# A recurrence's tables and matrices made inside the layers and kept in DRAM, and the second block's sums and low parts all on VectorE

## The chip, the cores and the metric

The kernel runs on one core of one Trainium2 chip. The metric is the device time of one execution in microseconds (us); before the change it is 1783.88 us, the median of 3 runs (1783.5 to 1784.17).

## The reference, cut to what matters

The model has two blocks. The first has two layers, each with three branches (a Mamba-2 scan, a sliding-window attention, a forgetting attention), gates and projections. The second has one layer with an S5 recurrence, a top-k sparse attention, a memory attention, and then a mixture of experts of 32 experts. All inputs are float32, there are 256 tokens of width 1024. The change touches how the S5 recurrence gets its constants:

```python
def s5_branch(u, lam_re, lam_im, log_dt, b_re, b_im, c_re, c_im, d_skip, w_glu):
    lam = lax.complex(lam_re, lam_im)
    dt = jnp.exp(log_dt)[:, None]
    lam_bar = jnp.exp(lam * dt)
    b_bar = ((lam_bar - 1.0) / lam)[..., None] * b
    bu = jnp.einsum('bsgh,gph->bsgp', uf, b_bar)
    _, states = lax.associative_scan(_ssm_combine, (a, bu), axis=1)
    y = jnp.real(jnp.einsum('bsgp,ghp->bsgh', states, c))
    ...
# then, in the same layer: sparse attention, memory attention, three gated up-projections, w_out,
# and hier_moe: for each of 32 experts silu(t @ w_gate[e]) * (t @ w_up[e]) @ w_down[e]
```

Nothing of `lam`, `dt`, `b`, `c` or `positions` depends on the first block, so the constants of the recurrence can be made at any time.

## The kernel before, in words

**Projections.** A weight piece of 512 KB is loaded into `wraw` (5 buffers). ScalarE copies it to the rounded high part `whi` (`wsplit`, L213 to L219) and the low part `wlo` (4 buffers) is the difference; TensorE then runs three matmuls per product (`proj_tok`, `proj_fm`). The difference is taken by VectorE (DVE), or by GpSimd (POOL) for one piece in `share[0]`. SyncE's queue (SP) issues all loads in one order; a load into `wraw` waits until the low part of the piece five before it is done.

**Order.** Each block is a string of steps (`ORDER1` for the two layers, `ORDER2` for block 2), read by `run_steps`. `name,args/k` sets a knob: in block 2 every fourth low part goes to POOL (`SH2 = 4`) or as `/k` says, and for `b` (a recurrence step) the bits of k put the sums before the scans (F, bit 2) and after them (E, bit 1) on POOL. A scheduler then orders each engine's queue by these steps' priorities and its own costs; weight loads get a higher priority.

**The recurrence.** Step `sa` (`sin_args`) makes sines and cosines of all angles on DVE and ScalarE, `sp` (`s5_params`, class `S5`) the decay and the input factor, `prep,q` (L881) the two block-diagonal matrices of a quarter: DVE products, PE transposes (L907, L914) and ScalarE copies. `b,q,i` (`block`, L920) is one of 16 recurrence steps: POOL makes a rotation table of 128 x 512 with three instructions (L937 to L939), PE multiplies, DVE rotates (L949 to L952), scans twice (L954, L955) and rotates back (L956 to L960). `end,q` sums a quarter. Every big tile here is a `unit` of 4 KB per partition, of which there are 16.

**The experts.** `fetch` loads their weights, 384 pieces of 512 KB, into a ring of slots: two tiles of a pool `early`, 6 units, 4 `wx`, the buffers of `wraw`, `whi`, `wlo`, `Thi`, `Tlo` and one row. `ahead,2` at the start and `ahead,6` at the end of `ORDER2` fetch the first 8 pieces; the others follow as slots come free, so most of the ring is filled when block 2 has used its last weights.

Of the kernel before, what the change touches and what calls it, by code (L numbers as in the profile page):

```python
# [45 lines left out]
SH1, SH2 = 0, 4  # L46
# [52 lines left out]
dt cq,1 cw cv,1 ax,0/6 cv,0 cq,0/3 ck,0 bk ck,1/6 ca,0,0 ca,1,0 ad,0 ax,1 ax,2 ca,1,1 g,2,1/6 ax,3/3 as_,0,0/0  # L99
z,2,1/0 ca,0,1 g,2,0/3 ad,1 bq,0/0 as_,0,1/3 z,2,0/0 p,2,0/1 bq,1/0 as_,1,0/2 as_,1,1/2 br,0/1 p,2,1/0 z,0,1/6  # L100
br,1/1 ba,1,0 ba,0,0 ba,0,1 g,0,1 g,1,0/3 z,0,0/6 g,1,1 z,1,0/2 ba,1,1 g,0,0/2 p,0,0/0 z,1,1/4 p,0,1 p,1,0/0
p,1,1/1
""", """
cw cv,1 dt cq,1/6 ck,0 cq,0 ck,1 cv,0/2 bq,0/3 g,2,0 ax,1/2 g,2,1/6 ca,0,0 ca,1,0 bq,1 ca,0,1 ax,2/0 ax,0 z,2,0
ax,3 ad,0 ca,1,1 ad,1 as_,0,0/1 as_,0,1/3 z,2,1 as_,1,0 g,1,0/3 bk/3 br,0 br,1/1 as_,1,1 z,0,0 ba,0,0 p,2,1/0
z,0,1/6 ba,0,1 p,2,0/1 ba,1,0 g,0,1/3 ba,1,1 z,1,1/4 z,1,0/2 g,1,1 g,0,0 p,0,1/0 p,0,0 p,1,0/1 p,1,1/1
# [15 lines left out]
def tile_model(ctx: ExitStack, tc: tile.TileContext, I: dict, out: bass.AP):  # L122
# [7 lines left out]
    early = ctx.enter_context(tc.tile_pool(name="early", bufs=1, side="right"))  # L130
# [269 lines left out]
    def layer(l):  # L400
# [308 lines left out]
        def pr(i, c):  # L709
# [6 lines left out]
            def ev_p(t, ps):  # L716
# [3 lines left out]
                else:  # L720
# [6 lines left out]
                     z=z, g=gate, p=pr)  # L727
# [15 lines left out]
    def sin_args():  # L743
# [22 lines left out]
        rows = wtile([128, 128], F32, name="s5rows", bufs=1)  # L766
# [3 lines left out]
        ld = wtile([128, 2], F32, name="s5ld", bufs=1)  # L770
# [19 lines left out]
        tsm = wtile([128, 2, 16], F32, name="tsm", bufs=1)  # L790
# [23 lines left out]
        cs = wtile([128, 1440], F32, name="cs", bufs=1)  # L814
# [23 lines left out]
    def s5_params(cs, lam, dt):  # L838

        r = wtile([128, 16], F32, name="s5r", bufs=1)  # L840
        V.tensor_mul(r, lam[:, 0], dt)
        exp_acc(r, r)
        nt = wtile([128, 4, 16], F32, name="s5cs", bufs=1)
# [4 lines left out]
        f = wtile([128, 2, 16], F32, name="s5f", bufs=1)  # L848
# [14 lines left out]
    class S5:  # L863


        def __init__(self, cs, r, f):
            self.cs, self.r, self.f = cs, r, f
            self.bT, self.h = {}, {}
            self.pm = wtile([128, 2, 2], F32, name="s5pm", bufs=1)
            nc.sync.dma_start(self.pm.rearrange("p a b -> p (a b)"), I["c_cmask"])  # L870
            self.dsk = wtile([128, 4], F32, name="s5d", bufs=1)
            nc.sync.dma_start(self.dsk, I["d_skip_2"][0].rearrange("(q p) -> p q", p=128))
# [5 lines left out]
        def start(self, u_fm):  # L878
            self.u = u_fm

        def prep(self, q):  # L881

            bs = wtile([128, 2, 4, 16], F32, name="s5b")
            cr = wtile([128, 2, 64], F32, name="s5c")
# [5 lines left out]
            tb = wtile([128, 4, 64], F32, name="s5t", bufs=1)  # L890
# [11 lines left out]
            bT = self.bT[q] = unit().rearrange("p (k n) -> p k n", k=8)  # L902
            bb8 = self.bb.rearrange("p i c n -> p (i c) n")
            for k0 in (0, 4):
# [3 lines left out]
                S.copy(bT[:, k0:k0 + 4, :], tp)  # L908
            z = wtile([128, 2, 2, 64], F32, name="s5z", bufs=1)
# [8 lines left out]
            self.h[q] = [unit() for _ in range(2)]  # L918

        def block(self, q, i):  # L920
            j = 4 * q + i
            E, F = (G if knob[0] & m else V for m in (1, 2))
            full = [128, 2, 16, 16]
            cs = self.cs
# [14 lines left out]
            G.tensor_tensor(tw, tw, tx, op=OP.add)  # L939
            two = [128, 2, 256]  # L940
# [73 lines left out]
    def rope2(dst, src, cs, t, nh):  # L1014
        c, s = (cs[:, k + 512 + 32 * t:k + 544 + 32 * t][:, None, :].to_broadcast([128, nh, 32]) for k in (256, 848))
# [54 lines left out]
    def block2(pair=None):  # L1070
        W = I["w_in_2"][0]
        mpair = xT = xf = kmT = vm = u_fm = s5 = wm = wf = par = None
# [51 lines left out]
        def ev_kv(t, ps):  # L1124
# [3 lines left out]
            rope2(kk[:, 0:1], kn[:, None, :], par[0], t, 1)  # L1128
# [4 lines left out]
            rope2(qr[t][:, 512:768].rearrange("p (h d) -> p h d", h=4), qn.rearrange("p (h d) -> p h d", h=4), par[0], t, 4)  # L1133
# [3 lines left out]
            rope2(kk[:, 0:1], kin[:, None, :], par[0], t, 1)  # L1137
# [167 lines left out]
        def ahead(n):  # L1305
            for _ in range(n):
# [4 lines left out]
                     mn=memory_norm, wm=norm_weights, sa=sines, sp=states, lo=finish_layer, nt=normed, kv=memory_kv,  # L1311
# [8 lines left out]
        for c in range(2):  # L1320
# [13 lines left out]
                 e=lambda: early.tile([128, 1024], F32, name="we", bufs=RAWE),  # L1334
# [427 lines left out]
```

## Time and profile before

| | |
|---|---|
| median of 3 runs | 1783.88 us |
| the profiled execution | 1783.39 us, span 1781.5 us, so 1.9 us lie around the span |
| layers (two of them) | 46 to 960 us of the span |
| block 2 up to the router | 960 to 1310 us |
| experts | 1310 to 1781 us |
| busy: PE, DVE, ACT, POOL | 94%, 56%, 39%, 17% of the span |
| the chain that ended last, by engine | PE 69%, DMA 17%, DVE 9%, POOL 2% |

The busy shares are means over stages with different limits: PE is busy all the time in the layers, DVE has its highest share in block 2, and the DMA queues are full from 1310 us on. So each stage is read by itself below. In the rows, "PE proj L149" is a matmul that accumulates into a tile `proj` and is issued by line 149; `u` is any unit.

### The profile page before, as it was taken

What the parts mean: (1) busy time and instruction counts of PE and PEld (TensorE: products, weight loads), DVE (VectorE), ACT (ScalarE), POOL (GpSimd) and SP (SyncE); (2) the same over time, 40 slices, a digit from 0 to 9 for tenths busy, and PEclk for the clock granted to TensorE, in tenths of its full rate; (3) what the DMA queues carried; (4) which work ended last, traced back from release to release, by engine and by line L of the source; (5) the groups of instructions that cost most, each with busy time, mean ns of one, the idle gap of its engine ahead of it and who ended that gap; (6) DMA issues with size and microseconds to landing.
All of it is one profiled execution on the core that took longest, in us unless ns stands there. A gap on an engine that the chain in (4) does not pass through costs nothing.

```text
span 1781.5 us, 23994 instructions
## 1 busy us (share of the span) xinstructions
PE 1680.2 (94%) x8941; PEld 1245.8 (70%) x8941; DVE 997.4 (56%) x1642; ACT 695.9 (39%) x1331; POOL 297.4 (17%) x242
## 2 busy tenths in 40 slices
PE   7999999999999999999998997887879999999998
PEld 6999888888798999888876876764634443434342
DVE  6656656666673568675668797899631221212121
ACT  5455555644444656556536553311311110101010
POOL 0111116220102101321013423374100000000000
PEclk9999999999999999999999998998989999999999
DMA  8644445455566544453565543123799999999997
GB/s 268 197 143 138 135 148 147 144 166 165 166 175 180 168 118 132 137 165 108 186 198 152 146 141 95 48 71 106 248 409 376 410 409 409 409 409 409 409 409 300
DMA packets 185592, 389.65 MB, mean 219 GB/s; under 512 B 28736, under 2 KB 65792, under 8 KB 185472
## 3 DMA queue, kind: packets, MB, share of 16 engines
q1 hardware_dynamic: 185472, 388.08, 64.0%
q8 instruction: 72, 1.18, 0.3%
q14 instruction: 48, 0.39, 0.1%
HBM read 386.98 MB, written 1.05 MB: 218 GB/s over the span
## 4 chain that ended last, share of the span: by engine, by line
PE 69%; DMA 17%; DVE 9%; POOL 2%; issue 2%; ACT 1%; SPq 0%; DVEq 0%; ACTq 0%; POOLq 0%
PE proj L149 45%; PE proj L1574 6%; PE sc L149 5%; PE pv L149 4%; PE sc L1596 3%; DMA Tlo<-in_w_up_dram 2%; DMA whi<-in_w_up_dram 2%; DMA wx<-in_w_up_dram 2%; DMA wraw<-in_w_down_dram 2%; PE tp L386 1%; PE tp L305 1%; DMA u<-in_w_up_dram 1%; DMA u<-in_w_down_dram 1%; DMA wlo<-in_w_up_dram 1%; DVE wlo L217 1%
## 5 line engine op out<-in xcount | busy, mean ns | idle before, releaser
L217 DVE TENSOR_TENSOR wlo<-wraw,whi 128x1024 fp32r<-128x1024 f32 (+1 forms) x278 | 361.0, 1302 | 173.9 <-PE proj L149 120.6
L216 ACT CAST whi<-wraw 128x1024 fp32r<-128x1024 f32 x322 | 337.4, 1051 | 284.1 <-PE proj L149 228.6
L149 PE MATMUL proj<-whi,Thi 128*128 128x512 f32 (+1 forms) x1008 | 396.1, 396 | 11.2 <-ACT u L1277 8.7
L149 PE MATMUL proj<-wlo,Thi 128*128 128x512 f32 (+1 forms) x1008 | 398.5, 396 | 4.0 <-DVE wlo L217 2.5
L149 PE MATMUL proj<-whi,Tlo 128*128 128x512 f32 (+1 forms) x1008 | 394.7, 394 | 0.0
L149 PEld LDWEIGHTS proj<-whi,Thi 128*128 128x128 f32 x1008 | 190.7, 189 | 50.0 <-ACT u L1277 8.9
L149 PEld LDWEIGHTS proj<-wlo,Thi 128*128 128x128 f32 x1008 | 190.6, 189 | 43.5 <-DVE wlo L217 5.7
L149 PEld LDWEIGHTS proj<-whi,Tlo 128*128 128x128 f32 x1008 | 190.5, 189 | 37.7
L217 POOL TENSOR_TENSOR wlo<-wraw,whi 128x1024 fp32r<-128x1024 f32 (+1 forms) x44 | 111.5, 2534 | 404.7 <-PE proj L149 299.8
L149 PE MATMUL proj<-Thi,whi 128*128 128x256 f32 x560 | 158.2, 287 | 2.3 <-DVE u L489 1.6
L149 PE MATMUL proj<-Thi,wlo 128*128 128x256 f32 x560 | 159.0, 285 | 0.0
L149 PE MATMUL proj<-Tlo,whi 128*128 128x256 f32 x560 | 158.2, 285 | 0.0
L1578 DVE SCALAR_TENSOR_TENSOR th<-th,cg,proj 128x512 f32<-128x512 f32 x16 | 12.0, 747 | 212.8 <-PE proj L1574 210.7
L149 PEld LDWEIGHTS proj<-Thi,whi 128*128 128x128 f32 x560 | 107.3, 193 | 3.5 <-DVE u L489 1.8
L149 PEld LDWEIGHTS proj<-Thi,wlo 128*128 128x128 f32 x560 | 108.1, 193 | 0.2
L149 PEld LDWEIGHTS proj<-Tlo,whi 128*128 128x128 f32 x560 | 107.3, 193 | 0.1
L149 PE MATMUL sc<-u 128*128 128x256 f32 (+1 forms) x416 | 98.7, 353 | 6.8 <-DVE u L950 6.4
L1577 ACT ACTIVATE th<-proj,cg 128x512 f32<-128x512 f32 x16 | 11.0, 687 | 191.2 <-PE proj L1574 191.2
L1600 DVE TENSOR_TENSOR u<-sc,u 128x512 fp32r<-128x512 f32 x32 | 22.0, 691 | 109.5 <-ACT u L1599 90.4
L149 PEld LDWEIGHTS sc<-u 128*128 128x128 f32 x416 | 69.1, 194 | 15.2 <-issue 8.7
L377 ACT ACTIVATE P<-sc,nm 128x256 f32<-128x256 f32 (+1 forms) x152 | 63.7, 432 | 38.7 <-DVE nm L370 24.3
L1599 ACT CAST u<-sc 128x512 fp32r<-128x512 f32 x32 | 18.6, 585 | 136.1 <-PE sc L1596 113.5
(467 smaller groups left out, 2537.9 us busy)
## 6 DMA issues: line engine op xcount, KB each, us to landing
wraw<-in_w_in_dram SPq DMA_DIRECT2D x236, 512.0 KB, 3.8
wraw<-in_w_proj_dram SPq DMA_DIRECT2D x48, 512.0 KB, 4.2
u<-in_w_up_dram SPq DMA_DIRECT2D x25, 512.0 KB, 10.2
wraw<-in_w_out_dram SPq DMA_DIRECT2D x24, 512.0 KB, 4.7
u<-in_w_gate_dram SPq DMA_DIRECT2D x24, 512.0 KB, 10.2
wraw<-in_w_up_dram SPq DMA_DIRECT2D x21, 512.0 KB, 10.2
whi<-in_w_down_dram SPq DMA_DIRECT2D x21, 512.0 KB, 10.2
u<-in_w_down_dram SPq DMA_DIRECT2D x21, 512.0 KB, 10.2
```

Of the source, the lines that this page charges most:

```text
L149: T.matmul(o, l, r, start=start, stop=stop)
L216: S.copy(hi[:, :, :n], raw[:, :, :n])
L217: (G if share[0] and scount[0] % share[0] == 0 else V).tensor_sub(lo[:, :, :n], raw[:, :, :n], hi[:, :, :n].bitcast(F32))
L305: T.transpose(ps[:, b, :], src[:, b * 128:(b + 1) * 128], ident)
L377: S.activation(P[:, i * nS:(i + 1) * nS], scv[:, i, :], AF.Exp, bias=nm[:, i:i + 1], accum_out=l_out[:, i:i + 1])
L386: T.transpose(tp[:, j, :], P[:, j * 128:(j + 1) * 128], ident)
L1574: pin(T.matmul(ps[r], xk, w[:, 512 * j:512 * j + 512], start=k == 0, stop=k == 7))
L1577: S.activation(hid, pg, AF.Silu, scale=cg[:, 1:2])
L1578: V.scalar_tensor_tensor(hid, hid, cg[:, 0:1], pu, op0=OP.mult, op1=OP.mult)
L1596: pin(T.matmul(po[c][r], hT[:, k, r], w[:, 512 * c:512 * c + 512], start=k == 0, stop=k == 3))
L1599: S.copy(yh[:, c], po[c])
L1600: V.tensor_sub(yl[:, c], po[c], yh[:, c].bitcast(F32))
```

## The change

- `sin_args` and `s5_params` run in layer 0 (`sa`, `sp`), with tiles of a pool `s5` on the right side of the memory instead of `early`.
- A class `Made` has the steps `cl` (two memsets), `mat,q` (the old `prep`, which then writes the two matrices of 512 KB each to DRAM) and `turn,j` (the three POOL instructions of a rotation table, then a write of 256 KB to DRAM). `mat,0` to `mat,3` and `turn,0` to `turn,7` stand in layer 0, `turn,8` to `turn,15` in layer 1.
- In block 2 `prep,q` loads the two matrices and `block` loads its table (`s5rot`, 3 buffers); the constants of the position rotation are loaded too.
- `SH2` is 0 and `ORDER2` has no `/k`: every low part and every sum of block 2 is on DVE. The three gated sums of L1298 stay on POOL.
- `early` is opened after the layers, where `s5` lay.

```diff
-SH1, SH2 = 0, 4
+SH1, SH2 = 0, 0
 ORDER1 = ["""
-dt cq,1 cw cv,1 ax,0/6 cv,0 cq,0/3 ck,0 bk ck,1/6 ca,0,0 ca,1,0 ad,0 ax,1 ax,2 ca,1,1 g,2,1/6 ax,3/3 as_,0,0/0
+dt cq,1 cw sa cv,1 sp cl ax,0/6 mat,0 cv,0 mat,1 cq,0/3 mat,2 ck,0 mat,3 bk ck,1/6 ca,0,0 ca,1,0 ad,0 turn,0 ax,1
...
 ORDER2 = """
-ahead,2 mn sa sp lo wm nt kv prep,0 u/6 b,0,1/1 keys/6 vk mem_q sel,0 queries/3 mem,0 b,0,0/3 gate,2,1/6 mem,1 b,0,3/1
+ahead,2 mn sp lo wm nt kv prep,0 u b,0,1 keys vk mem_q sel,0 queries mem,0 b,0,0 gate,2,1 mem,1 b,0,3
...
-    early = ctx.enter_context(tc.tile_pool(name="early", bufs=1, side="right"))
+    dram = ctx.enter_context(tc.tile_pool(name="dram", bufs=1, space=bass.MemoryType.DRAM))
+    made = ExitStack()
+    sp = made.enter_context(tc.tile_pool(name="s5", bufs=1, side="right"))
+    early = []
...
+    class Made:
+        def __init__(self):
+            self.rot = [dram.tile([128, 1024], F32, name=f"rot{n}") for n in range(8)]
+            self.mats = [dram.tile([128, 2, 1024], F32, name=f"mats{n}") for n in range(4)]
+            self.misc = dram.tile([128, 144], F32, name="misc")
...
+        def mat(self, q):
...
+            nc.sync.dma_start(self.mats[q][:, 0], bT)
...
+            nc.sync.dma_start(self.mats[q][:, 1], czf)
+        def turn(self, j):
...
+            tw = sp.tile([128, 512], F32, name="s5tw", bufs=1)
+            tx = wtile([128, 512], F32, name="th")
...
             G.tensor_tensor(v4(tw), pairs(256, 592), ca, op=OP.mult)
             G.tensor_tensor(v4(tx), pairs(0, 256), sa, op=OP.mult)
             G.tensor_tensor(tw, tw, tx, op=OP.add)
+            nc.sync.dma_start(self.rot[j // 2][:, 512 * (j % 2):512 * (j % 2) + 512], tw)
...
+        def prep(self, q):
+            b, c = unit(), wtile([128, 1024], F32, name="s5cz", bufs=1)
+            nc.sync.dma_start(b, made_.mats[q][:, 0])
+            nc.sync.dma_start(c, made_.mats[q][:, 1])
...
+        def block(self, q, i):
+            j = 4 * q + i
+            E, F = (G if knob[0] & m else V for m in (1, 2))
+            tw = wtile([128, 512], F32, name="s5rot", bufs=3)
+            nc.sync.dma_start(tw, made_.rot[j // 2][:, 512 * (j % 2):512 * (j % 2) + 512])
...
+    made_ = Made()
     with scoped("b1"):
         layer_out(0, layer(0))
         pair = layer(1)
     lay.close()
+    made.close()
+    early.append(ctx.enter_context(tc.tile_pool(name="early", bufs=1, side="right")))
```

POOL's queue in the middle of block 2, before: tables (L937 to L939), low parts (L217) and the sums before and after the scans (L951, L952, L959, L960) by turns.

```order
L315 TENSOR_TENSOR rstd_10042<-rstd,neghalf 128x8
L937 TENSOR_TENSOR u<-cs 128x512
L938 TENSOR_TENSOR u<-cs 128x512
L939 TENSOR_TENSOR u<-u 128x512
L951 TENSOR_TENSOR u<-u 128x256
L952 TENSOR_TENSOR u<-u 128x256
L217 TENSOR_TENSOR wlo<-wraw,whi 128x1024
L959 TENSOR_TENSOR u<-u 128x256
L960 TENSOR_TENSOR u<-u 128x256
```

The same place after: the last norms, then only the gated sums and the memsets of the expert stage.

```order
L319 TENSOR_TENSOR rstd_10103<-rstd,neghalf 128x4
L319 TENSOR_TENSOR rstd_10239<-rstd,neghalf 128x8
L319 TENSOR_TENSOR rstd_10257<-rstd,neghalf 128x8
L1336 TENSOR_TENSOR u<-u 128x512 x4
L1465 MEMSET wts 128x1 x8
```

All tables, low parts and sums have left POOL's queue there (the numbers behind `rstd` name the tile).

POOL's queue in layer 0 after: `s5tw` is the table's single buffer, so the first product of a table (L949) waits until the table before it has been written to DRAM.

```order
L221 TENSOR_TENSOR wlo<-wraw,whi 128x1024
L951 TENSOR_TENSOR s5tw<-s5tw,th 128x512
L949 TENSOR_TENSOR s5tw<-cs 128x512
L951 TENSOR_TENSOR s5tw<-s5tw,th 128x512
L949 TENSOR_TENSOR s5tw<-cs 128x512
L498 MEMSET u 64x1024 x2
L221 TENSOR_TENSOR wlo<-wraw,whi 128x1024
```

Behind the waiting product stand the memsets of the keys (L498) and a low part; before the change nothing of the tables stood in this part of the queue.

SP's queue in layer 0 after, with the writes of matrices (`mats`) and of the first two tables (`rot`):

```order
L923 DMA mats_102<-u 128x1024
L932 DMA mats_102<-u 128x1024
L902 DMA u<-in_c_im_dram 128x64
L205 DMA wraw<-in_w_in_dram 128x2x512
L952 DMA rot_94<-s5tw 128x512
L205 DMA wraw<-in_w_in_dram 128x2x512 x2
L901 DMA u<-in_b_re_dram 128x4x16
L902 DMA u<-in_c_re_dram 128x64
L901 DMA u<-in_b_im_dram 128x4x16
L902 DMA u<-in_c_im_dram 128x64
L923 DMA mats_103<-u 128x1024
L932 DMA mats_103<-u 128x1024
```

Weight loads (`wraw`) now stand behind writes that wait for ScalarE's copies and POOL's tables.

## Rows read from the trace of the kernel before

**Rows 1.** Busy time by stage: width, each engine, PE clock, DMA share and rate.

```profile
core 0: us, PE busy (x) PEld busy (x) DVE busy (x) ACT busy (x) POOL busy (x), PEclk, DMA share, GB/s
46.00:484.00 438.00, 432.88 (x2542) 382.32 (x2542) 279.67 (x389) 237.32 (x456) 82.48 (x61) 1.00 0.52 155
520.00:960.00 440.00, 438.17 (x2548) 385.29 (x2548) 284.75 (x443) 239.62 (x464) 75.58 (x52) 1.00 0.53 157
960.00:1310.00 350.00, 291.51 (x1333) 225.59 (x1332) 283.54 (x546) 132.14 (x271) 130.36 (x116) 0.93 0.44 138
1180.00:1200.00 20.00, 20.00 (x76) 13.42 (x75) 17.27 (x22) 1.45 (x3) 16.34 (x15) 1.00 0.18 51
1310.00:1490.00 180.00, 173.76 (x864) 75.26 (x865) 35.75 (x74) 18.83 (x34) 0.00 (x0) 0.98 1.02 401
1490.00:1781.00 291.00, 274.45 (x1216) 113.54 (x1212) 56.83 (x104) 27.40 (x48) 0.00 (x0) 0.99 0.99 393
```

**Rows 2.** Chain of waits, block 2, shares of the stretch by line.

```profile
by line: PE proj L149 29.4%; PE pv L149 5.3%; PE sc L149 4.7%; issue 4.4%; DVE wlo L217 4.4%; DVE u L957 3.4%; DVE u L955 3.2%; DVE u L956 2.4%; DVE u L951 2.1%; DVE u L952 2.1%; DVE u L949 2.0%; DVE u L950 1.9%; DVE u L954 1.9%; DMA wraw<-
```

**Rows 3.** Chain of waits, pieces: start us, length us, what.

```profile
967.92 0.68 DVE u L809
...
968.76 1.20 DVE x L1068
...
973.87 0.70 ACT cs L815
...
989.61 0.87 PE tp L1055 x8
...
1083.07 1.00 DVE u L901
1084.08 1.32 DVE u L901
```

**Rows 4.** Single instructions of DVE: start us, length us, line, operation.

```profile
963.45 3.41 DVE L1068 SCALAR_TENSOR_TENSOR x<-x,rstd,rowb 128x1024 f32<-128x1024 f32 x1 [0.24 <-POOL rstd L315]
...
1205.09 0.68 DVE L949 TENSOR_TENSOR u<-sc,u 128x512 f32<-128x512 f32 x1
...
1206.75 0.42 DVE L952 TENSOR_TENSOR u<-u 128x256 f32<-128x256 f32 x1
...
1210.39 0.68 DVE L949 TENSOR_TENSOR u<-sc,u 128x512 f32<-128x512 f32 x1
...
1212.89 1.48 DVE L952 TENSOR_TENSOR u<-u 128x256 f32<-128x256 f32 x1
...
1217.60 0.68 DVE L949 TENSOR_TENSOR u<-sc,u 128x512 f32<-128x512 f32 x1
```

**Rows 5.** Single instructions of POOL, the same stretch.

```profile
1211.63 1.06 POOL L938 TENSOR_TENSOR u<-cs 128x512 f32<-128x512 f32 x1
```

**Rows 6.** DVE groups of block 2: shape, count, busy us, mean ns, idle before.

```profile
L217 DVE TENSOR_TENSOR wlo<-wraw,whi 128x1024 fp32r<-128x1024 f32 x38 | 52.8, 1399 | 6.5 <-PE proj L149 4.9 <-ACT whi L216 1.0 <-issue 0.5
```

**Rows 7.** POOL groups of block 2.

```profile
L217 POOL TENSOR_TENSOR wlo<-wraw,whi 128x1024 fp32r<-128x1024 f32 x10 | 26.1, 2609 | 40.0 <-ACT whi L216 34.3 <-PE proj L149 5.8
L939 POOL TENSOR_TENSOR u<-u 128x512 f32<-128x512 f32 x16 | 21.3, 1334 | 1.1
L938 POOL TENSOR_TENSOR u<-cs 128x512 f32<-128x512 f32 x16 | 20.4, 1276 | 0.0
L937 POOL TENSOR_TENSOR u<-cs 128x512 f32<-128x512 f32 x16 | 19.7, 1234 | 53.4 <-DVE u L957 14.4 <-DVE u L1295 13.8 <-DVE u L960 13.5
```

**Rows 8.** Who waited for whom, block 2: us in total, times, longest.

```profile
DVE u L949 <- POOL u L939: 8.0, 3, 3.0
...
PE tp L914 <- ACT u L908: 4.8, 1, 4.8
```

**Rows 9.** SP's queue over the whole span: waits.

```profile
SPq L201 <- DVE wlo L217: 591.2, 185, 16.8
```

**Rows 10.** DMA issues: KB each, median us to landing.

```profile
out_dram<-x SPq DMA_DIRECT2D x4, 256.0 KB, 3.1
```

More of the change, by code (lines that the diff above doesn't have):

```diff
@@ L726, in layer @@
         steps = dict(dt=a_steps, cw=a_conv, ck=c_k, cq=c_q, cv=c_v, ca=c_att, ax=a_x, ad=a_dt, as_=a_ssd, bq=b_q, bk=b_kv, br=b_rope, ba=b_att,
-                     z=z, g=gate, p=pr)
+                     z=z, g=gate, p=pr, sa=made_.sines, sp=made_.states, cl=made_.clear, mat=made_.mat, turn=made_.turn)
         run_steps(ORDER1[l], steps, SH1)
@@ L876, in __init__ @@
             G.memset(self.cz, 0.0)
[L878 to L884, printed above, removed]
+        def mat(self, q):
+            u = unit()
+            bs = u[:, 0:128].rearrange("p (c i h) -> p c i h", c=2, i=4)
+            cr = u[:, 128:256].rearrange("p (c d) -> p c d", c=2)
+            tb = u[:, 256:512].rearrange("p (c n) -> p c n", c=4)
+            z = u[:, 512:768].rearrange("p (c a d) -> p c a d", c=2, a=2)
             for c, (b_, c_) in enumerate((("b_re_2", "c_re_2"), ("b_im_2", "c_im_2"))):
@@ L917, in prep @@
             S.copy(dst, tp[:, 0:2, :].rearrange("p c (i n) -> p c i n", i=4))
[L918 to L922, printed above, removed]
+            nc.sync.dma_start(self.mats[q][:, 1], czf)
+        def turn(self, j):
+            cs = self.cs
             full = [128, 2, 16, 16]
-            cs = self.cs
             def pairs(k0, stride):
@@ L939, in block, with __init__, start @@
             G.tensor_tensor(tw, tw, tx, op=OP.add)
+            nc.sync.dma_start(self.rot[j // 2][:, 512 * (j % 2):512 * (j % 2) + 512], tw)
+    class S5:
+        def __init__(self):
+            self.bT, self.cz, self.h = {}, {}, {}
+            self.rr = wtile([128, 144], F32, name="s5m", bufs=1)
+            nc.sync.dma_start(self.rr, made_.misc)
+            self.rope, self.r = self.rr[:, 0:128], self.rr[:, 128:144]
+            self.dsk = wtile([128, 4], F32, name="s5d", bufs=1)
+            nc.sync.dma_start(self.dsk, I["d_skip_2"][0].rearrange("(q p) -> p q", p=128))
+        def start(self, u_fm):
+            self.u = u_fm
+        def prep(self, q):
+            b, c = unit(), wtile([128, 1024], F32, name="s5cz", bufs=1)
+            nc.sync.dma_start(b, made_.mats[q][:, 0])
+            nc.sync.dma_start(c, made_.mats[q][:, 1])
+            self.bT[q] = b.rearrange("p (k n) -> p k n", k=8)
+            self.cz[q] = c.rearrange("p (c i n) -> p c i n", c=2, i=4)
+            self.h[q] = [unit() for _ in range(2)]
+        def block(self, q, i):
[3 more added lines that the diff above has]
+            nc.sync.dma_start(tw, made_.rot[j // 2][:, 512 * (j % 2):512 * (j % 2) + 512])
             two = [128, 2, 256]
@@ L1082, in norm_weights @@
             wm = unit_row(I["g_mix_2"][0])
-        def sines():
-            nonlocal par
-            par = sin_args()
         def states():
             nonlocal s5
-            s5 = S5(par[0], *s5_params(*par))
+            s5 = S5()
         def finish_layer():
@@ L1310, in block2 @@
                      vk=positions, ahead=ahead,
-                     mn=memory_norm, wm=norm_weights, sa=sines, sp=states, lo=finish_layer, nt=normed, kv=memory_kv,
+                     mn=memory_norm, wm=norm_weights, sp=states, lo=finish_layer, nt=normed, kv=memory_kv,
                      u=inputs, **{n: lambda *a, n=n: getattr(s5, n)(*a) for n in ("prep", "block", "end")})
```

98 lines of the change are left out of this document (49 added, 49 removed).

## The prediction, made before the changed kernel ran

> **What bounds the kernel now.** I read the busy time by stage first [rows 1]. In the two layers PE is busy 432.9 of 438 us and 438.2 of 440: they are PE-bound, and DVE (64%) and POOL (17 to 19%) work beside it. In block 2 (960 to 1310 us) PE is busy 291.5 of 350 us, DVE 283.5 and POOL 130.4, and PE's granted clock is 0.93 on the mean (stretches at 1.2 GHz between those at 2.4): no engine is full, they wait for each other. From 1310 us on the DMA queues are full (share 1.02 and 0.99, 401 and 393 GB/s), and the chain that ended last runs through weight loads; PE isn't full (274.5 of 291 us). The 384 expert pieces come in one stream that starts when block 2's last weights free their buffers, so the end moves with block 2's end, one for one: a us won in block 2 or lost in the layers is a us of the total.
>
> Then the chain of waits in block 2 [rows 2]: nearly half of it is DVE. The recurrence's lines (L949 to L957) have 1.9 to 3.4% of 350 us each, the low parts 4.4%. Last the single instructions [rows 4, 5]. A recurrence step whose table is not made meanwhile takes 5.30 us on DVE (first rotation at 1205.09, that of the next step at 1210.39) and has all its ten instructions there. The next step, with POOL's table instructions beside it (one at 1211.63), takes 7.21 us (1210.39 to 1217.60): L952 is 1.48 us long instead of 0.42. So POOL's work makes DVE's longer, and this is the reader's main point.
>
> **The change part by part: block 2.**
>
> - Tables gone from POOL: three instructions of 1.234, 1.276 and 1.334 us, 16 times, 61.4 us in all [rows 7]. What they cost is their hold on DVE: 7.21 − 5.30 = 1.91 us a step. L949 has 2.0% of 350 us on the chain, 7.0 us, at 0.64 us visible of each: 11 of the 16 steps lie on it. 11 × 1.91 = 21.0 us. The sums that move from POOL to DVE are in this already, since the 5.30 us step has them all. But in 1180 to 1200 us PE is busy 20.0 of 20 us [rows 1]: what DVE saves there is hidden behind PE, about 3 steps, −5.7 us.
> - DVE's waits for a table, 8.0 us in 3 [rows 8]: gone, if the loads (below) are early.
> - The start of the block: the final norm's L1068 is 3.41 us beside a POOL low part and 1.20 us the next time [rows 3, 4], 2.2 us; two pieces of the sine tables on the chain, 0.68 and 0.70 us. Together 3.6 us.
> - `prep` leaves: PE's wait before L914, 4.8 us [rows 8], and two DVE products on the chain, 1.00 and 1.32 us [rows 3]: 7.1 us.
> - Against it: 11 low parts come from POOL to DVE (10 whole, one smaller). 11 × 1.399 = 15.4 us of DVE [rows 6]. Of DVE's 52.8 us of low parts 15.4 us (4.4% of 350) are on the chain, 29%, so 4.5 us.
>
> Waits removed: 21.0 − 5.7 + 8.0 + 3.6 + 7.1 − 4.5 = 29.5 us. PE's clock comes on top: 7% of 350 us are 24.5 us of lost work, beside 58.5 us in which PE is idle, 0.42 us for each idle one. Part of the low-clock time is idle anyway, so I take half of 29.5 × 0.42: 6 us. Block 2: 35.5 us shorter. Bounds: 8 us (half of the steps that PE doesn't cover, 15.3 us, and nothing else) to 58.5 us (all of PE's idle time).
>
> New in block 2 are loads of 16 tables of 256 KB and 8 matrices of 512 KB, 8 MB; at 401 GB/s some 21 us of the queues, whose share is 0.44 there [rows 1]: room enough. They stand in SP's one queue between weight loads, and a table waits for a buffer whose recurrence step is done. Behind such a wait stand `wraw` loads, and PE waits for those. SP waits for low parts in this way already, 591.2 us in 185 waits, 3.2 us each, and PE hardly notices, since five pieces are loaded ahead [rows 9]. I put 0 on it, 26 us (8 of the 24 loads at 3.2 us) as the bad end.
>
> **The layers.**
>
> - 41 transposes (10 per quarter and one for the parameters) come to PE where it is full. Eight take 0.87 us [rows 3]: 41 × 0.109 = 4.5 us, nearly sure.
> - POOL gets 61.4 us of tables. In the layers PE is idle 5.1 + 1.8 = 7.0 us beside 158.1 us of POOL [rows 1], 0.044 us for each; 61.4 × 0.044 = 2.7 us. The bad end: each of the 16 tables delays one POOL low part by its length, 2.609 us [rows 7], and PE with it: 42 us. Below nothing it can't be, since nothing leaves the layers. I take 2.7, as the row of the same stage.
> - The matrices are now made between DVE, PE, ScalarE and SP early in layer 0. Before, one of the four made PE wait 4.8 us [rows 8]; I take the same once. The ends are 0 and 4 × 4.8 = 19 us. DVE has room for the sines and products: 158 of 438 us are free in the layer [rows 1].
> - A table's first product waits until the last table is written, since there is one buffer. A write of 256 KB takes 3.1 us to land [rows 10]; behind the waiting product stand memsets of the keys and low parts, and PE waits for those when the write is late. Within the 42 us above.
>
> The layers: 4.5 + 2.7 + 4.8 = 12.0 us longer.
>
> **Sum.** 35.5 − 12.0 = 23.5 us. The profiled execution is 1783.39 us (span 1781.5 and 1.9 around it): 1759.9 us. The median shown is 0.5 us above the profiled one, so 1760 us.
>
> **The rivals.**
>
> A, PE becomes the bound and the layers hide all but the transposes. For it: POOL's 130 us leave nearly all, and DVE then has under 270 us to do in block 2 (283.5, less 16 × 1.91 = 31, plus 15.4; `prep` and the sines go too) against PE's 291.5. Against: single chains stay (last recurrence step, `end`, `glu`, the router). Price: the 29.5 us and half of the other 29 us of idle time, 44 us; 1783.4 − 44 + 4.5 = 1744 us.
>
> B, slower: the hold on DVE only moves. POOL's tables meet the low parts of the layers, and there PE has no time to spare. If each of the 16 tables costs PE one POOL low part, 42 us, the layers grow by 4.5 + 4.8 + 42 = 51 us: 1783.4 − 35.5 + 51 = 1799 us. It decides from (35.5 − 9.3) / 16 = 1.6 us a table on. For it: L952's 1.48 us. Against: DVE is idle a third of the layers and POOL four fifths, and PE waits there only 0.044 us per us of POOL. The Trainium skill states such a rule ("SBUF — State Buffer", section "Who interferes with whom"): a DVE instruction with two SBUF inputs and a GpSimd instruction that reads SBUF exclude each other, and the one that comes second is blocked for the whole of the other. The low part has two SBUF inputs, so by that rule the layers pay each table that falls on a due low part; the trace agrees as to L952, while L949, which reads PSUM, stays at 0.68 us beside POOL.
>
> C, the gain is lost inside block 2: table loads make SP late. 35.5 − 26 us there, and the layers' 12.0: 1786 us. For it: one queue. Against: the 3.2 us above, and PE's loads five pieces ahead.
>
> **How the numbers follow.** A change under 0.2% (3.6 us) can't be told from none in this kernel. My forecast, with the sizes as above (1748 to 1776 us), has 0.61; A 0.16; B 0.12; C 0.11, of which half ends within 0.2% and the rest on both sides, slower a little more. Faster 0.79, same 0.07, slower 0.14. The forecast is 1760 us. The range goes to 1740 below, A's time less 4, which leaves 0.07 out, and to 1784 above, which leaves out B and half of C's, some 0.14.
>
> **What would show it.** Right: in block 2 PE busy over 90% at a clock near 0.97, recurrence steps of 5.3 us each, POOL under 30 us, no wait of DVE for a table; layers 8 to 16 us longer, by transposes and one or two waits of PE early in layer 0; the stream of experts shifted as a whole, at the same 390 to 400 GB/s. B shows as PE waiting for low parts (L217's successor) beside table instructions in the layers. C shows as waits of SP for a recurrence step with PE waiting for `wraw` behind it. I am wrong if block 2 shrinks by less than 20 us, or if the layers grow by more than 20.

## The result, and the profile after

The changed kernel takes 1765.46 us (median of 4 runs, 1762.19 to 1768.05) against 1783.69 us for the one before (4 runs, 1782.51 to 1784.17): a ratio of 0.9898, 95% interval 0.9877 to 0.9918. The profiled execution is the 1762.19 us one, its span 1760.4 us. 1760 us was forecast.

Busy time by stage in the changed kernel (width, each engine, PE clock, DMA share and rate); it answers to [rows 1]:

```profile
46.00:484.00 438.00, 424.32 (x2503) 375.72 (x2502) 297.31 (x470) 236.35 (x463) 125.71 (x96) 0.98 0.55 167
520.00:960.00 440.00, 437.32 (x2628) 387.98 (x2627) 286.54 (x411) 238.15 (x463) 83.75 (x56) 1.00 0.55 165
...
1310.00:1490.00 180.00, 176.34 (x876) 75.46 (x877) 37.55 (x75) 20.92 (x36) 0.00 (x0) 1.00 1.02 404
1490.00:1760.00 270.00, 252.32 (x1118) 103.99 (x1114) 51.95 (x97) 25.00 (x44) 0.00 (x0) 0.99 0.98 391
```

The first layer has lost PE time (432.88 busy before, 424.32 now), the second has not, and the expert stream runs at the rate it had. To see where the time went I numbered the matmuls of the helper's line (L149 before, L153 after; 6222 in both traces) by their starts, set each against the one of the same number, and took the difference. Inside block 2 the order is not quite the same (5600 and 6000 fall on other tiles), so those two columns compare how far the work has come; the others fall on the same tiles:

```
matmul no.             200   400   600  1600  2600  4000  4800  5000  5200  5600  6000  6221
before, us            48.8  77.9 107.0 275.1 501.8 721.0 889.1 941.2 998.3 1102  1227  1307
after, later by       +2.7 +20.0 +22.3 +22.3 +24.3 +24.3 +25.9 +23.9 +14.4  -0.2 -18.4 -20.7
```

So there are two large sums of opposite sign. Layer 0 loses 22.3 us over the work that the kernel before has done at 107 us, and the difference then stays. From the block's head (matmul 5000) to the router (6221), 366.0 us become 321.5: block 2 wins 44.6 us. (Two us more are won between 4800 and 5000, where two of block 2's low parts stood on POOL; the layers' loss is 25.9 us ahead of them and 23.9 behind.) The same stretch of both kernels, before and then after:

```profile
941.00:1307.00 366.00, 309.06 (x1416) 239.90 (x1414) 297.30 (x576) 142.14 (x284) 134.55 (x119) 0.94 0.44 138
```

```profile
965.00:1286.50 321.50, 296.94 (x1375) 232.51 (x1373) 250.44 (x510) 132.04 (x266) 20.43 (x35) 0.97 0.55 178
```

PE's idle time falls from 56.9 to 24.6 us, POOL from 134.6 to 20.4, and the clock rises from 0.94 to 0.97. The recurrence in the changed kernel, DVE's single instructions, answers to [rows 4]:

```profile
1194.36 0.69 DVE L991 TENSOR_TENSOR u<-sc,s5rot 128x512 f32<-128x512 f32 x1
...
1196.02 0.42 DVE L994 TENSOR_TENSOR u<-u 128x256 f32<-128x256 f32 x1
...
1199.65 0.68 DVE L991 TENSOR_TENSOR u<-sc,s5rot 128x512 f32<-128x512 f32 x1
```

A step is 5.29 us, and L994 (L952 before, where it took 1.48 us) is 0.42. The waits in block 2 and on SP's queue over the span answer to [rows 8, 9]:

```profile
PE pv L153 <- DMA s5cz<-mats: 3.0, 1, 3.0
```

```profile
SPq L205 <- DVE wlo L221: 564.5, 197, 14.5
...
SPq L981 <- DVE u L999: 38.4, 10, 6.6
SPq L952 <- POOL s5tw L951: 30.2, 13, 4.0
```

No wait for a table's making is left; the loads cost PE one wait of 3.0 us. DVE's low parts in 960 to 1310 us are 60 of mean 1209 ns now. [rows 6] has 38 of 1399 in that window, but the block has moved in it and this view counts two forms; in the stretch from matmul 5000 to 6221 there were 45 on DVE and are 57, the 12 of POOL's, and a whole one takes 1217 ns in place of 1382:

```profile
L221 DVE TENSOR_TENSOR wlo<-wraw,whi 128x1024 fp32r<-128x1024 f32 (+1 forms) x60 | 71.9, 1209 | 12.4 <-PE proj L153 10.6 <-issue 1.3 <-ACT Thi L310 0.4
```

Layer 0 is the other side. Who made PE wait from 40 to 90 us:

```profile
PE tp L921 <- DVE u L915: 6.4, 1, 6.4
PE proj L153 <- DVE u L788: 2.8, 1, 2.8
PE proj L153 <- DVE s5dt L833: 2.2, 1, 2.2
PE proj L153 <- DVE wlo L221: 1.0, 1, 1.0
```

The kernel before waits 1.6 us there. The first wait is for a matrix (L915 puts its entries in place, and the transposes at L921 follow in PE's order), the next two for DVE's work on the projections behind the sines' and parameters' small operations: they end at 50.5 and 57.8 us, each some 0.15 us after the last of three reads of `proj` on DVE (L536), among which the small operations stand. With the waits goes the clock. The two stretches before, then after:

```profile
30.00:60.00 30.00, 28.40 (x180) 25.70 (x179) 25.00 (x42) 14.39 (x20) 2.38 (x1) 1.00 0.82 250
60.00:90.00 30.00, 30.00 (x223) 28.71 (x222) 15.53 (x17) 14.21 (x19) 7.12 (x4) 1.00 0.64 191
```

```profile
30.00:60.00 30.00, 23.98 (x134) 21.05 (x133) 24.20 (x74) 11.04 (x15) 4.30 (x3) 0.92 0.70 201
60.00:90.00 30.00, 23.54 (x132) 20.94 (x132) 25.60 (x59) 12.85 (x18) 9.35 (x6) 0.85 0.38 110
```

0.92 and 0.85 against 1.00 are 2.4 + 4.5 = 6.9 us of work. 12.4 − 1.6 of waiting and 6.9 of clock leave 4.6 of the 22.3 us, about what 40 transposes take at 0.109 us each (4.4). Before the longest wait, POOL and DVE:

```profile
76.76 1.41 POOL L949 TENSOR_TENSOR s5tw<-cs 128x512 f32<-128x512 f32 x1 [2.35 <-ACT cs L822]
78.14 2.06 POOL L950 TENSOR_TENSOR th<-cs 128x512 f32<-128x512 f32 x2
80.16 2.33 POOL L221 TENSOR_TENSOR wlo<-wraw,whi 128x1024 fp32r<-128x1024 f32 x1
82.46 1.25 POOL L951 TENSOR_TENSOR s5tw<-s5tw,th 128x512 f32<-128x512 f32 x1
```

```profile
79.26 0.97 DVE L857 TENSOR_TENSOR s5cs<-s5cs,s5lam 128x16 f32<-128x16 f32 x1
80.27 2.27 DVE L859 TENSOR_TENSOR s5cs<-s5cs 128x16 f32<-128x16 f32 x1
82.57 1.18 DVE L860 TENSOR_TENSOR s5f<-s5cs,s5dt 128x16 f32<-128x16 f32 x1
83.67 0.16 DVE L862 TENSOR_TENSOR s5cs<-s5cs,s5lam 128x16 f32<-128x16 f32 x1
```

An operation on 128x16 numbers (L859, 0.165 us in the kernel before) takes 2.27 us beside POOL's low part of 2.33: it waits for nearly the whole of the other.

### The profile page after: what moved, and what is told of

The parts are those of the page before. It is cut to its first block, busy times and chain, and to the rows that moved or that the text cites. A ratio compares the mean times of both kernels' runs of the same rounds, so it can differ in the third digit from the quotient of the medians.

```text
span 1760.4 us, 24091 instructions
## 1 busy us (share of the span) xinstructions
PE 1677.4 (95%) x8941; PEld 1246.4 (71%) x8941; DVE 987.2 (56%) x1678; ACT 695.0 (39%) x1331; POOL 242.6 (14%) x206
## 4 chain that ended last, share of the span: by engine, by line
PE 73%; DMA 15%; DVE 8%; POOL 1%; issue 1%; ACT 1%; SPq 0%; DVEq 0%; POOLq 0%; ACTq 0%
PE proj L153 48%; PE proj L1612 6%; PE sc L153 5%; PE pv L153 4%; PE sc L1634 3%; DMA whi<-in_w_up_dram 2%; DMA wx<-in_w_up_dram 2%; DMA Tlo<-in_w_up_dram 2%; PE tp L390 1%; PE tp L309 1%; DVE wlo L221 1%; PE tp L1571 1%; DMA u<-in_w_down_dram 1%; DMA wraw<-in_w_down_dram 1%; DMA wlo<-in_w_up_dram 1%
## 5 line engine op out<-in xcount | busy, mean ns | idle before, releaser
L221 DVE TENSOR_TENSOR wlo<-wraw,whi 128x1024 fp32r<-128x1024 f32 (+1 forms) x292 | 374.1, 1286 | 172.0 <-PE proj L153 118.7
L153 PE MATMUL proj<-wlo,Thi 128*128 128x512 f32 (+1 forms) x1008 | 397.8, 395 | 0.0
L153 PE MATMUL proj<-whi,Thi 128*128 128x512 f32 (+1 forms) x1008 | 395.1, 395 | 1.0 <-ACT Thi L310 0.7
L153 PE MATMUL proj<-whi,Tlo 128*128 128x512 f32 (+1 forms) x1008 | 393.3, 393 | 0.0
L153 PEld LDWEIGHTS proj<-whi,Thi 128*128 128x128 f32 x1008 | 190.1, 189 | 39.4 <-ACT Thi L310 1.9
L153 PEld LDWEIGHTS proj<-whi,Tlo 128*128 128x128 f32 x1008 | 189.8, 188 | 37.6 <-DVE Tlo L311 0.2
L153 PEld LDWEIGHTS proj<-wlo,Thi 128*128 128x128 f32 x1008 | 190.1, 189 | 36.8
L153 PE MATMUL proj<-Thi,whi 128*128 128x256 f32 x560 | 160.7, 290 | 5.7 <-DVE u L788 2.8
L153 PE MATMUL proj<-Thi,wlo 128*128 128x256 f32 x560 | 161.2, 289 | 1.0 <-DVE wlo L221 1.0
L153 PE MATMUL proj<-Tlo,whi 128*128 128x256 f32 x560 | 160.8, 289 | 0.0
L221 POOL TENSOR_TENSOR wlo<-wraw,whi 128x1024 fp32r<-128x1024 f32 x30 | 77.4, 2580 | 315.0 <-PE proj L153 205.0
L153 PEld LDWEIGHTS proj<-Thi,whi 128*128 128x128 f32 x560 | 109.5, 197 | 7.0 <-issue 5.4
L153 PEld LDWEIGHTS proj<-Thi,wlo 128*128 128x128 f32 x560 | 110.0, 197 | 1.5 <-DVE wlo L221 1.3
L153 PEld LDWEIGHTS proj<-Tlo,whi 128*128 128x128 f32 x560 | 109.4, 196 | 0.1
L153 PE MATMUL sc<-u 128*128 128x256 f32 (+1 forms) x416 | 97.1, 349 | 3.8 <-DVE u L992 3.8
L153 PEld LDWEIGHTS sc<-u 128*128 128x128 f32 x416 | 68.4, 192 | 11.2 <-issue 4.6
L381 ACT ACTIVATE P<-sc,nm 128x256 f32<-128x256 f32 (+1 forms) x152 | 63.8, 433 | 31.6 <-DVE nm L374 17.4
```

The costliest lines, as they stand in the source:

```text
L153: T.matmul(o, l, r, start=start, stop=stop)
L221: (G if share[0] and scount[0] % share[0] == 0 else V).tensor_sub(lo[:, :, :n], raw[:, :, :n], hi[:, :, :n].bitcast(F32))
L381: S.activation(P[:, i * nS:(i + 1) * nS], scv[:, i, :], AF.Exp, bias=nm[:, i:i + 1], accum_out=l_out[:, i:i + 1])
```

## The experiments

Each was timed in 4 to 12 runs against 9 to 17 of the kernel before on the same chip. "Later by" is the matmul count above, from the profiled runs.

**One part alone, and the other.** The kernel before with this edit of the change (and no `/k` in ORDER2):

```diff
-SH1, SH2 = 0, 4
+SH1, SH2 = 0, 0
```

> The kernel before with one part of the change alone: block 2's sums (22.7 us on POOL before) and low parts of weights (68.4 us) all on DVE, the tables (73.1 us on POOL) still made in block 2, nothing in the layers. Theory 1: POOL's time beside DVE costs whoever makes it, so block 2 gives back in proportion to the POOL time that goes, 91 of 164 us: of the 40 us that block 2 lost in the changed kernel some 22, a time of 1762 us. Rival: the tables' chain is what block 2 waited for and the low parts on DVE fill the place that POOL left; then 5 us or less, 1779 us or more.

1776.77 us, ratio 0.9956 (0.9943 to 0.997): 7 us won, where theory 1 wanted 22 and its rival up to 5. (By the trace POOL had 20 us of sums, 28 of low parts and 61 of tables in block 2, less than the expectation took; by these theory 1 would want 18, and fails as well.) 3.6 us of the gain lie between 5000 and 6221, and 2.0 just ahead, where two low parts stood. The changed kernel with the opposite edit, so that the tables and matrices move alone:

> The changed kernel with the other part alone: tables and matrices made in the layers, but block 2's sums and low parts shared with POOL as before. Layers keep their cost of about 20 us. Theory 1: block 2 gives back in proportion to the 73 of 164 us of POOL time that go, some 18 us, plus the matrices' preparation, 7 us: 1783.7 + 20 - 25 = 1779 us. Rival (the tables' chain is what block 2 waited for): block 2 gives back 35 us or more, 1768 us or less.

1769.84 us, 0.9925 (0.9911 to 0.9939). The tables and matrices win 42.4 us from 5000 to 6221, nearly all of the 44.6; the layers cost 28.0. DVE's operations beside POOL's low parts and sums are 17.3 us longer in that stretch than alone, yet little of it reaches the end. A split in proportion to POOL's time is wrong: moving the tables and matrices out is the gain, and the sums and low parts add 2.2 us to it (4.4 by the medians). So the price of such a hold depends on where it falls; what makes these places cheap was not tested.

**Is it hold or chain?** The changed kernel with idle work on POOL in each step:

```diff
+            du = wtile([128, 512], F32, name="dum", bufs=1)
+            for _ in range(3):
+                G.tensor_tensor(du, tw, tw, op=OP.mult)
             two = [128, 2, 256]
```

> The changed kernel, and in each of block 2's sixteen steps three products 128x512 more on GpSimd, which read the loaded table and write a tile that nobody reads: 48 instructions of 1.1 to 1.4 us, some 60 us of GpSimd beside DVE, and no wait of anybody for them. Theory 1 (what tables in block 2 cost is mostly GpSimd's hold on DVE's operations): block 2 loses a good part of the 33 us that separate it from the kernel with the sums alone moved: 12 to 25 us, 1777 to 1790 us. Rival (it is the chain that waits for a table's products and for the matrices): 4 us or less, up to 1769 us.

1786.19 us, 1.0019 (1.0008 to 1.0029). Up to matmul 5000 it runs as the changed kernel does (+23.3), at 6221 it is 1.2 us later than the kernel before. So it wins 22.1 us in that stretch in place of 44.6: 22.5 us are lost, half of block 2's gain, to work that nobody waits for (20.7 by the medians). PE is idle 38.4 us of the stretch in place of 24.6, and its clock is 0.94 in place of 0.97. What it does to a step, DVE's instructions beside three of the products at 1205.41 to 1209.85:

```profile
1205.41 4.44 POOL L984 TENSOR_TENSOR dum<-s5rot 128x512 f32<-128x512 f32 x3 [3.81 <-DMA s5rot<-rot]
```

```profile
1206.16 1.35 DVE L1001 TENSOR_TENSOR u<-u,s5rot 128x512 f32<-128x512 f32 x1
1207.43 1.52 DVE L1002 TENSOR_TENSOR u<-u,s5rot 128x512 f32<-128x512 f32 x1
1209.06 1.07 DVE L1004 TENSOR_TENSOR u<-u 128x256 f32<-128x256 f32 x1
1210.06 0.41 DVE L1005 TENSOR_TENSOR u<-u 128x256 f32<-128x256 f32 x1
```

They are 0.68, 0.68 and 0.42 us alone. Over the stretch, DVE's operations beside POOL (each against the median of its line alone) are 22.8 us longer; in the kernel before 44.8, in the changed one 1.3. The same place with memsets in place of the products (`G.tensor_copy(du[:, 0:1], tw[:, 0:1])` and eight of `G.memset(du, 0.0)` a step):

> The changed kernel, and in each of block 2's sixteen steps a copy of one column and eight memsets 128x512 on GpSimd into a tile that nobody reads: by the memset 64x1024 of 0.95 us some 60 us of GpSimd again, as in the run with the idle products, but without reading a tile in the state buffer (but for the one column). Theory R (GpSimd holds DVE's operations only where it reads two tiles, as the products do): 3 us or less, up to 1768 us, and DVE's scans and sums keep 0.41 and 0.67 us beside a memset. Rival (any work on GpSimd slows DVE): again some 15 to 22 us, 1780 to 1787 us.

1768.39 us, 0.9917 (0.9903 to 0.993). POOL has 128 memsets of 0.525 us, 67 us in all, and DVE beside it:

```profile
1206.47 4.60 POOL L985 MEMSET dum<- 128x512 f32 x8
```

```profile
1207.04 0.69 DVE L1002 TENSOR_TENSOR u<-u,s5rot 128x512 f32<-128x512 f32 x1
1207.65 0.68 DVE L1003 TENSOR_TENSOR u<-u,s5rot 128x512 f32<-128x512 f32 x1
1208.37 0.42 DVE L1005 TENSOR_TENSOR u<-u 128x256 f32<-128x256 f32 x1
```

Not a tenth of a microsecond is lost. In the whole stretch only three operations of DVE beside POOL are more than 0.2 us longer than alone, and all three stand beside products of the gated sums, none beside memsets alone. It is POOL's reading that holds DVE, not its being busy. (From 5000 to 6221 this run loses 4.4 us, of which 3.3 are one wait of DVE for a memset; the median lies 2.9 us above the changed kernel's, within its runs' spread, and just over theory R's 1768.)

**The matrices in block 2.** The making of a matrix imitated in each `prep` of the changed kernel (nine DVE operations on a spare tile, `T.transpose` ten times, three `S.copy`; nobody reads the outcome):

> The changed kernel, and in each of block 2's four preparations the making of a matrix imitated on data that nobody reads: nine products and sums on DVE of the sizes of the old ones (128x64, 64x64, 128x256), ten transposes on PE, three copies on ScalarE. The kernel before lost 44.6 us more than this one from the block's head to the router; 9.5 of them lie in the head ahead of the first step, and the run with idle table products took 22.4 us back. Theory X (most of what is left, 13 us, is the matrices: PE's transposes wait in PE's order for DVE, and 4.5 us of the transposes themselves): 8 to 15 us lost, 1773 to 1781 us. Rival (only the transposes' own time; the rest is the tables' chain, whose products the rotations waited for): 3 to 6 us, 1768 to 1772 us.

1771.88 us, 0.9941 (0.9928 to 0.9955); 5.4 us lost from 5000 to 6221 in the profile, 6.4 by the medians. That is the rival's range: the transposes' 4.5 us and little more (PE is busy 4.6 us longer and idle 0.7). The 4.8 us of one wait before [rows 8] did not come back; the imitation has no tables beside it and leaves out the entries' loads, and which of these it would take is open.

**What costs the layers.** The first four tables later in layer 0's order (`turn,0` behind `g,2,1/6`, the next ones as far along):

> The changed kernel with the first four tables one to one and a half places later in layer 0's order, behind the attention's second steps; no work added or left out. Theory L (the layers' loss sits at one place, where the small DVE operations ahead of the last matrix take 1 to 2.3 us beside POOL's first table and a low part): the wait of 6.42 us at 79 us and the half clock behind it go, 6 to 9 us, 1757 to 1760 us. Rival H (POOL's hold costs the layers wherever the tables stand): the loss moves with the tables, within 3 us of 1765.

1765.6 us, 0.9894 (0.9879 to 0.991). This one tells nothing, because the edit didn't do what it says. The order is a priority, and POOL, which had nothing else, took the first table again as soon as the sines were there:

```profile
82.57 1.41 POOL L949 TENSOR_TENSOR s5tw<-cs 128x512 f32<-128x512 f32 x1 [2.35 <-ACT cs L822]
...
84.96 2.33 POOL L221 TENSOR_TENSOR wlo<-wraw,whi 128x1024 fp32r<-128x1024 f32 x1
```

So the work was taken out. Without the 48 table instructions and their stores (block 2 loads other data):

> The changed kernel with the 48 table instructions and their 16 stores left out of the layers; block 2 loads pieces of the same size and from DRAM in the tables' place, so the recurrence turns by wrong numbers. Theory L (the tables cost the layers nothing but in the one place beside the parameters at 76 to 84 us): 5 to 9 us less, 1756 to 1760 us. Rival H (POOL's hold follows the tables through the layers): the layers lose most of what they gained over before, 15 us or more, 1750 us or less.

1758.23 us, 0.9865 (0.9848 to 0.9882): 7.2 us for the tables. PE's wait before L921 is 3.01 us in place of 6.42, and behind matmul 600 the layers lose 1.4 us (20.1 to 21.5) in place of 3.6 (22.3 to 25.9). Rival H is out: outside of that one place, the tables cost the two layers some 2 us. Not that the hold had gone: from 46 to 930 us of the changed kernel, DVE's operations beside table instructions are 22.7 us longer than alone. It is there, and PE hardly waits for it. Without the matrices (`mat,0` to `mat,3` removed; wrong matrices are loaded):

> The changed kernel with the four matrices left out of layer 0 (their loads, products on DVE, 40 transposes and stores); block 2 loads weights of the same size in their place, so the recurrence runs on wrong matrices. Sines, parameters and tables stay. Theory W (what layer 0 loses is the matrices: 4.5 us of transposes, PE's wait of 6.42 us for DVE's entries and the half clock behind it): 12 to 17 us less, 1748 to 1753 us. Rival S (it is the sines' and parameters' small operations on DVE ahead of the projections' evictions and low parts): 4 to 9 us less, 1756 to 1761 us.

1757.38 us, 0.9855 (0.984 to 0.987): 8.1 us for the matrices by the medians, rival S's range. The waits of 2.2 and 2.9 us for the small operations stay. But the traces say more than 8.1. PE's wait for a low part at 43 us, ahead of every matrix, is 3.89 us in this run's profile and 0.95 in the changed kernel's; it varies among profiles with the same layer 0 (see the last section). Against the two with a long wait there (4.32 us in the run with the tables alone, 4.56 in the one with memsets, both 26.9 or 27.0 us late at matmul 600), this run's 14.1 is 12.8 us less, theory W's range. In the changed kernel's own trace the wait of 6.42 us and the transposes alone are 11 us. So the matrices are a third of the layers' loss by the medians and half of it by the traces, the sines and parameters most of the rest, and the runs do not settle between theories W and S.

**Another place.** Sines, parameters, matrices and first tables all behind the attention's first steps:

```diff
-dt cq,1 cw sa cv,1 sp cl ax,0/6 mat,0 cv,0 mat,1 cq,0/3 mat,2 ck,0 mat,3 bk ...
+... ax,1 sa ax,2 ca,1,1 g,2,1/6 sp cl ax,3/3 mat,0 as_,0,0/0 mat,1 z,2,1/0 ca,0,1 mat,2 turn,0 ...
```

> The changed kernel with sines, parameters, matrices and the first four tables all later in layer 0, after the attention's first steps instead of between the first projections; no work added or left out. Theory L: the four waits of PE before 84 us (0.95, 2.19, 2.80, 6.42 us) and the 13.6 us at half clock go, 12 to 19 us, 1746 to 1753 us, and layer 0 is longer than before by only the transposes' 4.5 us and little more. Rival H: the same work holds DVE and PE in another place, within 4 us of 1765.

1756.99 us, 0.9846 (0.9832 to 0.9859), between theory L's range and the rival's. The sines and parameters are nearly free there (+1.7 at matmul 1200), but the matrices then cost 15.7 us in place of the transposes' 4.5 (+17.4 at 1600; the profiled run is the slowest of the five, 3.4 us over their median, so the others may pay less here). The reason stands in DVE's row and in the windows behind it:

```profile
222.76 0.85 DVE L907 TENSOR_TENSOR u<-u,s5f 128x64 f32<-128x64 f32 x4 [4.75 <-DMA u<-in_b_re_dram]
```

```profile
215.00:220.00 5.00, 5.00 (x28) 4.22 (x27) 2.71 (x8) 1.54 (x3) 1.52 (x1) 1.00 0.98 302
220.00:225.00 5.00, 1.99 (x13) 1.34 (x12) 2.05 (x9) 1.51 (x3) 0.00 (x0) 0.92 0.98 330
225.00:240.00 15.00, 14.73 (x69) 14.30 (x70) 4.62 (x9) 8.59 (x24) 0.00 (x0) 0.50 0.06 19
```

DVE stands 4.75 us before the entries' load, with the queues 98% busy; PE's evictions (L311) stand behind it; PE is idle 3 us, and then works at 0.50 of its clock (1.2 GHz) for 15 us, 7.5 us of work. A place between the two:

> The changed kernel with the sines between the projections at 60 us, the parameters after them and the matrices one by one from the attention's first steps on (from about 105 us), the tables behind; no work added or left out. Theory L: layer 0 then pays the transposes' 4.5 us and one short wait; 1746 to 1753 us. If a matrix placed at any spot makes PE wait for its loads and for DVE, as in the run with all of it later (there 3 us of waiting and 16 us at half clock at 222 us, behind a DMA of 4.75 us): 1757 us or more.

1761.43 us, 0.9873 (0.9858 to 0.9888): not theory L but the other range. No half clock, but many small waits, 13.2 us of PE's time from 30 to 480 us (2.4 in the kernel before), 3.9 of them for entries of a matrix. The same with the raw entries loaded at the sines' step, in four transfers into one held tile:

> As the one before it, and the raw entries of the four matrices fetched in four transfers at the sines' step into one tile that is held, in place of four small transfers within each matrix. Theory M (in the run with all of it later, DVE stood 4.75 us before an entry's transfer while the queues were 98% busy, and PE behind DVE): no wait of DVE for a transfer there is left, 3 to 8 us less than the one before it if that one waits, and the same as it if it doesn't; 1745 to 1750 us. Rival: the transfers weren't what was late, but DVE's own work ahead of the matrices: no difference over 2 us.

1762.03 us, 0.9873 (0.9857 to 0.989): no difference, the rival's range. Theory M doesn't hold in this place; PE waits 4.5 us for DVE's entries all the same, and here the clock falls too (0.94 from 120 to 210 us). Last, the place of "all later", the early loads, and each matrix in two steps:

```diff
-mat,0 as_,0,0/0 mat,1 z,2,1/0 ca,0,1 mat,2 turn,0 g,2,0/3 ad,1 mat,3 ...
+mat,0 as_,0,0/0 z,2,1/0 mt,0 mat,1 ca,0,1 turn,0 g,2,0/3 mt,1 mat,2 ad,1 turn,1 bq,0/0 mt,2 mat,3 ...
```

with DVE's part in `mat` and the transposes, copies and stores in `mt`.

> As the run with all of it later, but each matrix in two steps (DVE's entries first, PE's transposes one or two steps of the layer behind them), and the raw entries loaded early into one held tile; the same work. Theory W2 (PE waits for a matrix because its transposes stand right behind DVE's entries in PE's order): no wait of PE over 1 us at a matrix and no half clock in layer 0, so the layers pay the 4.5 us of transposes and little more: 1744 to 1750 us. Rival (DVE has no slack for the added work wherever it stands, as the two placements before at 1761 and 1762 us suggest): 1755 us or more.

1751.38 us, 0.9824 (0.9809 to 0.984): the fastest, 14 us under the changed kernel (10.3 between the two profiled runs), and the intervals don't meet. Layer 0 loses 12.5 us (at 1600) in place of 22.3 and block 2 wins 45.1. Early layer 0 in the kernel before, in this version and in the changed kernel:

```profile
60.00:120.00 60.00, 60.00 (x431) 56.73 (x430) 31.08 (x34) 29.68 (x52) 12.39 (x11) 1.00 0.61 184
```

```profile
60.00:120.00 60.00, 60.00 (x430) 56.74 (x429) 31.09 (x34) 29.66 (x52) 12.40 (x11) 1.00 0.62 184
120.00:210.00 90.00, 88.58 (x605) 81.45 (x604) 76.54 (x172) 55.08 (x115) 20.71 (x13) 1.00 0.48 135
210.00:300.00 90.00, 87.14 (x481) 74.50 (x480) 56.05 (x80) 49.42 (x98) 31.45 (x24) 0.98 0.58 186
```

```profile
60.00:120.00 60.00, 53.19 (x351) 48.91 (x351) 44.04 (x97) 29.77 (x45) 19.09 (x15) 0.93 0.67 203
120.00:210.00 90.00, 90.00 (x666) 85.61 (x665) 57.79 (x92) 53.01 (x113) 5.79 (x7) 1.00 0.52 149
```

The 44 us of DVE from 60 to 120 us have become 31 again, and the clock stays at or near full. DVE's work stands from 120 to 210 us now: DVE is busy 76.5 of 90 us there, a fuller stretch than the 44 of 60, and PE is idle only 1.4 us at full clock. So it isn't DVE's share of a stretch that makes PE wait, but what of PE's work stands behind DVE there; what is different about this place was not tested. Theory W2 is met in part: one wait of 1.85 us for a matrix is left, the clock is 0.98 from 210 to 300 us, and layer 0 loses 12.5 us and not the transposes' 4.5 and little more. The time is 1.4 us above its range. Which of the two edits (early loads, split) made the difference to 1757 us, the runs don't say.

## Why the prediction was right, and where it was not

The forecast of 1760 us is 5.5 us under the median and 2 us under the profiled run. Its two sums were both too small, and of opposite sign: block 2 wins 44.6 us (35.5 forecast), the layers lose 23.9 (12.0). The errors of 9.1 and 11.9 us nearly cancel, and that is luck: the time came out closer than either part. By its own bound, "if the layers grow by more than 20", the layers' step failed. Block 2 came at rival A's price (44 us), with PE busy 92% of the stretch, but A's layers, which hide all but the transposes, did not come.

- **Tables' hold, 21.0 − 5.7 us.** Right in its mechanism, shown by the idle products: 22.5 us, clock included, and no operations made longer by memsets. The steps of 5.3 us came.
- **Waits for tables 8.0.** They are gone. Their price was not measured alone. Of the 44.6 us, the head (9.5), the products' hold (22.5), the imitated matrices (5.4) and the sums and low parts (2.2) would leave 5.0 us if they add up. No run shows that they do (the head holds some of the low parts), so what this wait cost stays open.
- **Start, 3.6.** It was 9.5 us (+23.9 to +14.4 from 5000 to 5200). The two halves of the change tell it apart: the sums and low parts alone win 2.0 us there (−2.3 to −4.3), near the 2.2 that I had put on the low part beside L1068, and the tables and matrices alone 6.8 (+28.0 to +21.2), where I had 1.4. I had counted two pieces of the sines, and not that sines and parameters leave the stretch as a whole.
- **`prep`, 7.1.** The imitation cost 5.4, most of it transposes. That the transposes, which I charged to the layers, leave block 2 too was missed.
- **Low parts on DVE, −4.5.** Wrong in sign: with the sums they win 2.2 us beside moved tables, 3.6 alone. POOL's low parts were 2.609 us each [rows 7] and held DVE as tables do: 12 came to DVE, but each of the 42 whole ones that DVE had took 0.165 us less (1382 to 1217 ns), some 7 us.
- **Clock, 6.** 0.94 to 0.97 of the stretch: 366 × 0.06 − 321.5 × 0.03 = 12 us, within 3 by the rounding. PE's busy time less the transposes fell by 12.1 − 4.5 = 7.6 us, nearer to the forecast.
- **Loads in block 2, 0.** One wait of 3.0 us for `s5cz`. Rival C did not come.
- **Transposes, 4.5.** Right: 0.109 us each at full clock; 4.6 us is what the waits and the clock leave.
- **Tables in the layers, 2.7 us.** Some 2 us outside one place, 7.2 us with it. Rival B's 42 us did not come: its hold did (22.7 us of DVE's time in the layers), but not its price, since PE waited for it in one place only. The Trainium skill's rule ("SBUF — State Buffer", section "Who interferes with whom") tells what is held, and the trace agrees with both sides of it: the page says that a GpSimd instruction that only writes SBUF doesn't contend with a DVE instruction that has two SBUF inputs, and the sums of 0.42 us took 1.07 beside products and 0.42 beside memsets. What it costs is told by the rows around it.
- **Matrices and sines making PE wait, 4.8 us.** The step that failed. I took the one wait of [rows 8] and called DVE's free third of the layer room enough. But the share was a mean: from 60 to 120 us, where most of the work was put, DVE went from 31 to 44 us, and from 43 to 86 us PE waited four times for DVE's reads of `proj`, low parts and entries, 12.4 us (1.6 before). I had no term for the clock in the layers: 6.9 us. Waits and clock are 17.7 us in place of the 4.8. And even the share of those 60 us would not have told it, since a fuller stretch of DVE left PE idle for only 1.4 us in the last version.

## What to carry to other kernels

Work moved into a full engine's shadow is not free by the mean share of the engine that does it; look at the window in which it will stand, and above all at who is queued behind it in order: DVE busy 73% of one window left PE idle for 6.8 us of 60, and 85% of another for 1.4 us of 90. Steps that end on a busy engine (here the transposes) are to stand some work behind those that feed them. A wait of 3 us on TensorE was followed by 15 us at half clock in one run, and one of 2.7 us by none in another, so short waits may cost more than their length and are to be priced with the clock in the rows behind them. And an edit of an order by priority is to be checked in the new trace, since an idle engine takes its work as early as before.

## What was unexpected

- The hold strikes small operations hardest: 2.27 us for one of 0.16 (128x16). The scans (`TENSOR_TENSOR_SCAN`) are held too, up to 1.52 us for 0.68 beside the idle products (1.75 beside a product of the gated sums), while the first rotation, which reads PSUM, keeps 0.66 to 0.68 us in every step in which it ran beside them.
- The changed kernel's own runs lie in two groups some 5 us apart (1762.19 and 1763.44; 1767.48 and 1768.05). Profiles with the same layer 0 differ as much by matmul 200 (+2.7 and +7.5): PE's wait for a low part at 43 us is 0.95 us in one and 4.6 in the other. What decides it was not found. It bears on every difference of a few us between two versions here, as in the run without the matrices.
